# Between out-projection and MLP of a hybrid decoder block: inputs in two sets of tiles, first MLP products among the last transposes, sums by operand, copies in a pool of their own

## The chip, the cores and the metric

The kernel runs on one core of a Trainium2 chip. The metric is the device time of one execution in microseconds. The profile is that of one execution, and its times are counted from the start of the profiled span. PE is TensorE (matmuls, and PEld its weight loads), DVE is VectorE, ACT is ScalarE, POOL is GpSimd, SP is SyncE, which here only issues DMAs.

## The reference

One decoder layer on x of 1024 rows (SEQ) by 1024 channels (D_MODEL), all in float32, with D_FF = 4096:

```python
def reference(x, ...):
    for l in range(DEPTH):            # DEPTH = 1
        h = rms_norm(x, norm_mix[l])
        x = x + hybrid_mixer(h, ...)  # ends with  y @ w_out
        h = rms_norm(x, norm_mlp[l])
        x = x + jnp.square(jax.nn.relu(h @ w_up[l])) @ w_down[l]
    return rms_norm(x, norm_final)
```

The mixer projects h to eight groups, runs two recurrences over the rows (RG-LRU and HGRN2), gates and adds their outputs to y, and multiplies y by w_out. The change concerns what lies between that multiplication and the first product of the MLP.

## The kernel before

**Precision.** A float32 operand is split in two fp32r parts: ACT copies it to the high part "H", DVE subtracts to get the low part "L" (`split`, L86 to L88). A product is three matmuls, H x H, L x H and H x L (`mm3`, L130 to L134).

**Products of the gates and the MLP.** Three stages (gates, MLP up, MLP down) use a recursive scheme with seven products in place of eight. The weights come in quads, 16 for each stage. A quad is loaded as two raw tiles of 512 KB (`load_quad`, L900). `quad_steps` (L905) makes its seven operands: "sums" adds four blocks on DVE into two more raw tiles s; "a" splits block A11 into the pool w1; "b", "c" and "d" split pairs of operands (s1 and s2, s3 and s4, A12 and A22) into tiles "w". There are four raw tiles (pool wp, tag raw) and six tiles w, which out-projection's weights use too. PLAN (L885) names for each step 0 to 6 the PSUM bank (X, Y, Z), the weight operand and the input operand: steps 0, 2, 4 and 6 accumulate in X, 1 and 5 in Y, 3 in Z. A product of one step is 12 matmuls of 128x512. After steps 0, 1 and 2 ACT copies the bank to a tile e; after steps 3, 4 and 5 DVE adds bank and copy into a tile b; after 6 the bank is the result.

**Stages in order.** (1) First norm and the mixer, eight interleaved stages (L873 to L883). (2) The remaining gates, quads 2 to 15 (L1072 to L1121), which read seven input operands: B11, B21 and B22 lie in memory already, t1, n2, T3 and T4 are loaded from DRAM by `load_combo`. `in_turn` chains these loads and the raw loads of the first quads on SP's queue. The gates write y to DRAM (yd). (3) Out-projection of the first 512 rows (`out_proj(0, ...)`, L1129), which reads y tiles loaded by `y_tiles(yp, 0)` and writes x2 to DRAM. (4) Out-projection of the other 512 rows, in two parts of two row tiles each (L1171 to L1193), with the second norm. (5) MLP up (`hidden`, L1215, and `hidden_ops`, L1240), quads 0 to 15. (6) MLP down and the last norm.

**The part around the change.** Row tiles tt = 0 to 3 stand for the rows of both halves: half 0 is row tile tt (loaded from DRAM as x2a), half 1 is row tile 4 + tt (x2s, just made by out-projection). In profile and prediction "tile 2" or "tile 3" is tt. `second_norm(tt, half)` (L1143) scales the row tile (`norm_rows`, L151: ACT squares and sums, DVE adds eps, POOL takes the power, DVE scales into xn), transposes it on PE in two groups of four 128x128 blocks (L1161, PSUM tag hg with two banks), copies the result on ACT to braw (L1162) and splits it into B11 and B21 (half 0) or B22 (half 1). At half 1 it also calls `combos` (L891: four additions on DVE), whose results are split into t1, n2, T3 and T4. Each input operand of the MLP thus has 512 columns, of which each tt makes 128, and a product needs all four. In (4) each part calls `second_norm(tt, 0)` for its two tiles, then two column halves hf of matmuls with eight weight tiles (`next_w`), adds the residual (L1190), stores x2 and calls `second_norm(tt, 1)`. x2a has one buffer. All of y's second half is read from four 1 MB tiles in the pool y1p.

After (4) the pools n2 and y1p close, and w1, ust and up open in their memory. Then quads 0 and 1 are loaded, A11 split, and steps 0 and 3 of both run first (L1256 to L1265); "c" of quad 0 and "sums" of quad 1 come at step 3, "b" and "c" of quad 1 after steps 5 and 6 of quad 0.

**What sets the order.** Each engine executes its instructions in a fixed order. The Tile framework's scheduler sets that order when the kernel is built, by program order as the priority and an estimate of when each instruction can run; `tc.high_priority(n)` moves instructions ahead, and `pin` (L126) keeps PE instructions in program order where `pinned[0]` is set. A tile of a pool that takes the memory of a closed pool waits for the last use of the tiles that lay there (`reuse_waits="tile"`).

Of the kernel before, what the change touches and what calls it, by code (L numbers as in the profile page):

```python
# [10 lines left out]
F32 = mybir.dt.float32  # L11
# [7 lines left out]
P = 128  # L19
# [25 lines left out]
def trunk(ctx: ExitStack, tc: tile.TileContext, x, wts, mlp, pv, gains, mask_f, mask_u, out):  # L45
# [358 lines left out]

    def conv(c, p, xc, xps):
        for s in range(2):
            u = 2 * p + s
            xp = xps[s]
            V.tensor_copy(xp[:, 0:3], xcar[:, u, :])
            for j in range(3):  # L410
                V.scalar_tensor_tensor(  # L411
                    xc[:, s, :],
                    xp[:, j : j + T],
                    pvt[:, PV_CW + 8 * j + u : PV_CW + 8 * j + u + 1],
                    xc[:, s, :],
                    op0=ALU.mult,
                    op1=ALU.add,
                )
            if c + 1 < NC:
# [79 lines left out]
    def hgrn(c, p, got, go):  # L499
# [111 lines left out]
        mul(pairs(kk)[:, :, 0, :], pairs(kc)[:, :, 0, :], t8[:, :, 1:2].to_broadcast([P, 16, 32]))  # L611
        mul(pairs(qf)[:, :, 1, :], q8[:, :, 1, :], t8[:, :, 0:1].to_broadcast([P, 16, 32]))
        level_blocks(0, c0, pt2)
# [145 lines left out]
    def stage(i):  # L759
# [19 lines left out]
        def convolve():  # L779
            got["xc"] = conv(c, p, xc, xps)  # L780

# [123 lines left out]
    def quad_steps(i, pools, raws=raw_tile, minus=False):  # L905
# [22 lines left out]
        def pair(src, names):  # L928
            def go():
                h, lo = (pools[1].tile([P, 1024], F32R, tag="w", name=f"w{names[0]}{i}{q}", bufs=6) for q in "HL")  # L930
# [128 lines left out]
    def ykt(c, ku):  # L1059
        p, s = divmod(ku, 2)  # L1060
        t = yt[c][p]
        s = s if c == 0 else 1 - s
        return t[:, 0, s, :], t[:, 1, s, :]

    def load_combo(o):
        for q in range(2):
            in_turn(gop[o][q].bitcast(F32), cd[o][:, q])
# [4 lines left out]
    for q in own[:2]:  # L1072
        load_quad(GQ + q, dma=in_turn if q == own[0] else load_late)
        gwork[q] = quad_steps(GQ + q, (w1p, wp), minus=True)
        with tc.high_priority(600):
            gwork[q]["a"]()
            if q == own[0]:
                gwork[q]["sums"]()
                gwork[q]["d"]()
    for o in ("t1", "n2"):  # L1080
        load_combo(o)
    in_turn(raw_q[GQ + own[1]][1], mlp[GQ + own[1], 1])
    for o in ("T3", "T4"):
        load_combo(o)
    pinned[0] = True
    for step in (0, 3):
        gate_step(own[0], step)
    pinned[0] = False
    gwork[own[0]]["b"]()
    gwork[own[0]]["c"]()  # L1090
# [3 lines left out]
    for q in own:  # L1094
        n = q + 1
        if n > own[1] and n < QUADS:
            gwork[n] = quad_steps(GQ + n, (w1p, wp), minus=True)
        for step in (1, 2, 4, 5, 6) if q == own[0] else (0, 1, 2, 3, 4, 5, 6):
# [4 lines left out]
            if q == own[0] and step == 2:  # L1103
                gate_step(own[1], 0)
# [13 lines left out]
            for k in {2: ("sums", "a", "b"), 5: ("c",), 6: ("d",)}.get(step, ()):  # L1118
                if q > own[0] or k != "a":
                    gwork[n][k]()  # L1120
        gate_work(q)  # L1121
    close_gp()
    close_tp()
    close_w1()
    close_hB()
    y1p, close_y = opened("y1p")
    y_tiles(y1p, 1)
    xsp, close_xs = opened("xs")
# [5 lines left out]
    HOME = {"T4": 0, "B22": 0, "T3": 0, "B21": 1, "n2": 2, "t1": 2, "B11": 3}  # L1134
    n2p, close_n2 = opened("n2")
    gain1 = gain_tile(1)
# [6 lines left out]
    def second_norm(tt, half):  # L1143
        cut = slice(tt * P, (tt + 1) * P)
        b = braw[tt, half] = n2p.tile([P, 2, T], F32, tag=f"b{half}", name=f"braw{tt}{half}", bufs=2 - half)
        t = tt + 4 * half
        xn = n2p.tile([P, D], F32, tag="xn", name=f"xn_h{t}", bufs=2)
        if half == 0:
            xs = n2p.tile([P, D], F32, tag="x2a", name=f"x2a{t}")
            nc.sync.dma_start(xs, x2d[t])  # L1150
        else:
            xs = x2s[tt]
        norm_rows(xs, xn, gain1, f"h{t}")

        def op_split(src, o):
            split(src.rearrange("p (k t) -> p k t", k=4), hop[o][0][:, :, cut], hop[o][1][:, :, cut])

        for h in range(2):
            pt = bank("hg", f"xT_h{t}_{h}")
            for k in range(4):  # L1160
                PE.transpose(pt[:, k * P : (k + 1) * P], xn[:, (4 * h + k) * P : (4 * h + k + 1) * P], ident)  # L1161
            A.copy(b[:, h, :], pt)  # L1162
            if (half, h) != (1, 0):
                op_split(b[:, h, :], {(0, 0): "B11", (0, 1): "B21", (1, 1): "B22"}[half, h])
        if half == 1:
            b0 = braw[tt, 0]
            combos(b0[:, 0, :], b0[:, 1, :], b[:, 1, :], b[:, 0, :])
            for src, o in ((b0[:, 0, :], "t1"), (b[:, 1, :], "n2"), (b[:, 0, :], "T3"), (b0[:, 1, :], "T4")):
                op_split(src, o)

    for part in range(2):  # L1171
# [5 lines left out]
        for hf in range(2):  # L1177
            pp = {tt: bank("pj", f"po1{hf}{tt}") for tt in tts}
            for j in range(4):
                wh, wl = next_w()  # L1180
                for k in range(2):
                    ku = 2 * j + k
                    yh, yl = ykt(1, ku)
                    cols = slice(k * 512, (k + 1) * 512)
                    for tt in tts:
                        cut = slice(tt * P, (tt + 1) * P)
                        mm3(pp[tt], yh[:, cut], yl[:, cut], wh[:, cols], wl[:, cols], ku == 0, ku == 7)
            for tt in tts:
                cols = slice(hf * 512, (hf + 1) * 512)
                V.tensor_tensor(out=x2s[tt][:, cols], in0=pp[tt], in1=x2s[tt][:, cols], op=ALU.add)  # L1190
        for tt in tts:
            nc.sync.dma_start(x2d[4 + tt], x2s[tt])
            second_norm(tt, 1)  # L1193
    close_n2()
    close_y()


    w1p, close_w1 = opened("w1")
    ust, close_ust = opened("ust")
    up, close_up = opened("up")  # L1200
    U_GROUPS = (("B11", "B21"), ("B22",), ("t1", "T4"), ("n2", "T3"))
    u_d = {
# [4 lines left out]
    u_ops = {}  # L1207
    work, b_of, bank_of, e_of = {}, {}, {}, {}

# [5 lines left out]
    def hidden(q, step):  # L1215
        bk, wo, ho = PLAN[step]
        first = (q, bk) not in bank_of
        if first:
            bank_of[q, bk] = bank(BANK[bk], f"u{bk}{q}")
        if q not in b_of:  # L1220
            b_of[q] = up.tile([P, 4, T], F32, tag="b", name=f"b{q}", bufs=2)
        o, b = bank_of[q, bk], b_of[q]
        wh, wl = ops_w[q][wo]
        hh, hl = hop[ho]
        for k in range(4):
            cols = slice(k * P, (k + 1) * P)
            mm3(o, wh[:, cols], wl[:, cols], hh[:, k, :], hl[:, k, :], first and k == 0, k == 3, not first)
        if step < 3:
            e_of[q, step] = up.tile([P, T], F32, tag="e", name=f"e{step}_{q}", bufs=4)
            A.copy(e_of[q, step], o)  # L1230
# [24 lines left out]

    for q in (0, 1):  # L1256
        load_quad(q)
        work[q] = quad_steps(q, (w1p, wp))
        work[q]["a"]()
        if q == 0:  # L1260
            work[0]["sums"]()
        work[q]["d"]()
        hidden(q, 0)
        hidden(q, 3)
    work[0]["b"]()  # L1265
    for q in range(QUADS):
# [3 lines left out]
        for step in range(7):  # L1270
            if q < 2 and step in (0, 3):
                if q == 0 and step == 3:
                    work[0]["c"]()
                    work[1]["sums"]()
                continue
            hidden(q, step)
            if q == 0:
                if step > 4:
                    work[1]["b" if step == 5 else "c"]()
                continue  # L1280
            if step == 1:
# [9 lines left out]
    late_u, close_late_u = opened("late_u", side="right")  # L1291
    hidden_ops(QUADS - 1, late_u, (2, 5), True)
    close_up()
    acc0, close_acc0 = opened("acc0", side="right")
# [170 lines left out]
```

## Time and profile before

| | |
|---|---|
| three runs of the kernel before | 1588.41 us median (1586.48 to 1588.73) |
| the profiled execution, its own time | 1585.07 us |
| its span | 1583.3 us |
| granted TensorE clock, mean | 0.992 |
| PE, DVE, ACT, POOL busy | 97%, 76%, 52%, 10% |
| DMA | 280.07 MB, mean 177 GB/s |

By stage PE's row of the 40 slices looks like this (a digit is the busy share of a slice of 39.6 us in tenths):

```profile
PE   7989999999999999999999978999999999999998
DVE  5797586696876938686856488988778888888877
```

The mixer takes the first 580 us, the gates 580 to 846, the out-projection of the first half 846 to about 893, the out-projection of the second half with the second norm up to 942, the MLP the rest. A row of the timeline reads: start, duration, engine, line, operation, output <- inputs, sizes, count, and in brackets how long the engine stood idle before it and what ended the wait. A row of the busy time by stage reads: stage, its length, busy time (instructions) of PE, PEld, DVE, ACT and POOL, granted TensorE clock, DMA share, GB/s. Matmul durations overlap, since matmuls are pipelined.

### The profile page before, as it was taken

What the parts mean: (1) busy time and instruction counts of PE and PEld (TensorE: products, weight loads), DVE (VectorE), ACT (ScalarE), POOL (GpSimd) and SP (SyncE); (2) the same over time, 40 slices, a digit from 0 to 9 for tenths busy, and PEclk for the clock granted to TensorE, in tenths of its full rate; (3) what the DMA queues carried; (4) which work ended last, traced back from release to release, by engine and by line L of the source; (5) the groups of instructions that cost most, each with busy time, mean ns of one, the idle gap of its engine ahead of it and who ended that gap; (6) DMA issues with size and microseconds to landing.
All of it is one profiled execution on the core that took longest, in us unless ns stands there. A gap on an engine that the chain in (4) does not pass through costs nothing.

```text
span 1583.3 us, 23131 instructions
## 1 busy us (share of the span) xinstructions
PE 1531.4 (97%) x9072; PEld 1278.8 (81%) x9072; DVE 1209.5 (76%) x1706; ACT 820.8 (52%) x1341; POOL 162.6 (10%) x187
## 2 busy tenths in 40 slices
PE   7989999999999999999999978999999999999998
PEld 6878888888788888888888767888888878888886
DVE  5797586696876938686856488988778888888877
ACT  5656756557475534454533376777677632211113
POOL 1021110234436600000000000000000000000000
PEclk9999999999999999999999999999999999999999
DMA  6223122232343375332328762766666675666652
GB/s 241 96 94 107 67 103 85 94 121 94 134 137 118 106 269 199 130 117 96 134 95 310 260 212 80 279 253 252 253 249 248 226 273 226 246 255 254 254 199 107
DMA packets 72205, 280.07 MB, mean 177 GB/s; under 512 B 7712, under 2 KB 16032, under 8 KB 59168
## 3 DMA queue, kind: packets, MB, share of 16 engines
q1 hardware_dynamic: 69072, 267.58, 45.3%
q10 hardware_dynamic: 3024, 11.01, 1.9%
q8 instruction: 71, 1.16, 0.3%
q14 instruction: 38, 0.31, 0.1%
HBM read 193.63 MB, written 84.93 MB: 176 GB/s over the span
## 4 chain that ended last, share of the span: by engine, by line
PE 76%; DVE 13%; ACT 6%; issue 2%; DMA 2%; POOL 1%; DVEq 0%; SPq 0%; POOLq 0%; ACTq 0%
PE dX L132 3%; PE dX L133 3%; PE uX L132 3%; PE dX L134 3%; PE uX L134 3%; PE gX L134 3%; PE gX L133 3%; PE uX L133 3%; PE gX L132 3%; PE uY L134 2%; PE gY L134 2%; PE gY L133 2%; PE uY L132 2%; PE uY L133 2%; PE gY L132 2%
## 5 line engine op out<-in xcount | busy, mean ns | idle before, releaser
L88 DVE TENSOR_TENSOR wL<-raw,wH 128x1024 fp32r<-128x1024 f32 x100 | 124.3, 1245 | 91.4 <-ACT wH L87 89.9
L87 ACT CAST wH<-raw 128x1024 fp32r<-128x1024 f32 x100 | 105.0, 1050 | 71.2 <-PE po L133 36.6
L1374 DVE TENSOR_TENSOR acc<-acc,dX 128x512 f32<-128x512 f32 x128 | 85.1, 685 | 29.3 <-PE dX L134 28.7
L87 ACT CAST wA<-q 128x512 fp32r<-128x512 f32 x46 | 28.4, 621 | 132.6 <-PE dX L134 101.4
L1374 DVE TENSOR_TENSOR acc<-acc,dY 128x512 f32<-128x512 f32 x64 | 43.5, 686 | 15.7 <-PE dY L134 14.5
L133 PE MATMUL po<-wL,y 128*128 128x512 f32 x128 | 50.0, 391 | 0.0
L134 PE MATMUL po<-wH,y 128*128 128x512 f32 x128 | 50.0, 391 | 0.0
L132 PE MATMUL po<-wH,y 128*128 128x512 f32 x128 | 49.8, 389 | 0.0
L1234 ACT ACTIVATE b<-b 128x512 f32<-128x512 f32 x48 | 30.2, 632 | 35.7 <-DVE b L1233 35.7
L155 POOL TENSOR_TENSOR rstd_h<-rstd_h,mhalf 128x1 f32<-128x1 f32 x8 | 5.5, 687 | 385.1 <-DVE rstd_h L154 385.1
L411 DVE SCALAR_TENSOR_TENSOR xc<-xp,pvt,xc 128x512 f32<-128x512 f32 x48 | 40.4, 864 | 0.0
L710 ACT ACTIVATE on<-po 128x128 f32<-128x128 f32 x64 | 16.9, 278 | 44.9 <-PE po L706 44.9
L88 DVE TENSOR_TENSOR wA<-q,wA 128x512 fp32r<-128x512 f32 x46 | 31.5, 686 | 10.3 <-ACT wA L87 10.3
L324 POOL TENSOR_TENSOR stt<-r,stt 128x256 fp32r<-128x256 f32 x16 | 23.2, 1467 | 93.1 <-ACT stt L323 93.1
L915 DVE TENSOR_TENSOR s<-q,q 128x512 f32<-128x512 f32 x46 | 31.6, 688 | 1.2 <-DMA q<-mlp_in 0.7
L920 DVE TENSOR_TENSOR s<-q 128x512 f32<-128x512 f32 x46 | 31.6, 687 | 0.4
L1235 ACT ACTIVATE b<-b 128x512 f32<-128x512 f32 x48 | 30.1, 631 | 1.1
L132 PEld LDWEIGHTS po<-wH,y 128*128 128x128 f32 x128 | 24.0, 188 | 5.0
L134 PEld LDWEIGHTS po<-wH,y 128*128 128x128 f32 x128 | 24.0, 188 | 4.9
L133 PEld LDWEIGHTS po<-wL,y 128*128 128x128 f32 x128 | 24.0, 188 | 4.9
L703 PE MATMUL po<-v,scT 128*128 128x128 f32 x128 | 24.7, 286 | 2.8 <-DVE sn L689 2.8
L616 POOL TENSOR_SCALAR scT<-dd 32x256 f32<-32x256 f32 x32 | 22.0, 687 | 50.4 <-DVE dd L532 48.9
(2528 smaller groups left out, 5422.6 us busy)
## 6 DMA issues: line engine op xcount, KB each, us to landing
raw<-wts_in SPq DMA_DIRECT2D x96, 512.0 KB, 3.4
q<-mlp_in SPq DMA_DIRECT2D x92, 512.0 KB, 3.5
y<-yd SPq DMA_DIRECT2D x7, 1024.0 KB, 8.7
x<-x_in SPq DMA_DIRECT2D x8, 512.0 KB, 6.0
hd<-ri SPq DMA_DIRECT2D x16, 256.0 KB, 2.7
od<-onT ACTq DMA_DIRECT2D x8, 512.0 KB, 4.4
cdT<-stT SPq DMA_DIRECT2D x16, 256.0 KB, 3.3
o<-od SPq DMA_DIRECT2D x4, 1024.0 KB, 7.3
```

Of the source, the lines that this page charges most:

```text
L87: keep(A.copy(h, src))
L88: keep(V.tensor_tensor(out=lo, in0=src, in1=h.bitcast(F32), op=ALU.subtract))
L132: pin(PE.matmul(o, ah, bh, start=first, stop=False, **how))
L133: pin(PE.matmul(o, ah, bl, start=False, stop=False, **how))
L134: pin(PE.matmul(o, al, bh, start=False, stop=last, **how))
L411: V.scalar_tensor_tensor(xc[:, s, :], xp[:, j : j + T], pvt[:, PV_CW + 8 * j + u : PV_CW + 8 * j + u + 1], xc[:, s, :], op0=ALU.mult, op1= ...
L703: pin(PE.matmul(on_ps, scT[:, 4 * s + n, :], vn(s, n), start=True, stop=only))
L915: V.tensor_tensor(out=sa[:, 0, :], in0=a21, in1=a22, op=ALU.add)
L920: V.tensor_tensor(out=sb[:, 0, :], in0=a21, in1=a11, op=ALU.add)
L1234: A.activation(b[:, at, :], b[:, at, :], AF.Relu, scale=-1.0 if at == 2 else 1.0)
L1235: A.activation(b[:, at, :], b[:, at, :], AF.Square)
L1374: V.tensor_tensor(out=dst, in0=dst, in1=banks[bk, pr], op=op)
```

## The change

- **Gates, first quads:** for quad 2 (the first) "b" is made ahead of "d" and under the same high priority, and the loads of t1, n2 and T3 stand ahead of the raw loads of quad 3. Quad 2's steps run in the order 1, 2, 5, 4, 6, and quad 3's first product follows step 4. The work on quad 3's operands gets a high priority.
- **Pools:** w1 and n2 open ahead of y1p and ahead of the out-projection.
- **Inputs in two sets:** y of the second half is loaded in eight tiles of 256 rows, four for part 0 (in n2) and four for part 1 (in y1p), instead of four tiles of 512 rows. Tiles that part 0 has read serve tt = 2 and 3 as x2a and as xn.
- **Norms:** the transposed rows are copied back into xn, braw has no tiles of its own; transposes are pinned where `pinned[0]` is set.
- **Sums by operand:** the four additions and the splits of t1, n2, T3 and T4 move from `second_norm` to a generator; they run after all four tiles' norms, t1 of every tile first, then n2, T3, T4.
- **Last part:** at part 1, hf 1, PE runs weights 0 and 1 for both tiles, then 2 and 3 for tile 2, then 2 and 3 for tile 3, pinned. Ahead of the last tile's matmuls `first_weights` loads quads 0 and 1 and makes "a" of both and "sums" and "b" of quad 0. After the matmuls PE runs product (quad 0, step 0), tile 2's transposes, product (quad 1, step 0), tile 3's transposes.
- **MLP start:** then "d" and "c" of quad 0 at high priority, and the steps of quad 0 in the order 3, 1, 2, 5, 4, 6, pinned, without those of quad 1, whose operands follow. The copies e get a pool `ep` of their own.
- `conv` gets a parameter that is None wherever it is called, and `got["wide"]` is stored and not read.

```diff
@@ second_norm
-        b = braw[tt, half] = n2p.tile([P, 2, T], F32, tag=f"b{half}", ...)
+        late = half == 0 and tt > 1
-        xn = n2p.tile([P, D], F32, tag="xn", name=f"xn_h{t}", bufs=2)
...
-            xs = n2p.tile([P, D], F32, tag="x2a", name=f"x2a{t}")
+            xs = n2p.tile([P, D], F32, tag=f"y0{2 * tt - 4}" if late else "x2a", name=f"x2a{t}")
...
+        home = {2: "y01", 3: "y03", 5: "x2a", 6: "y00", 7: "y02"}.get(t, "xn")
+        xn = n2p.tile([P, D], F32, tag=home, name=f"xn_h{t}", bufs=3 if home == "xn" else 1)
         norm_rows(xs, xn, gain1, f"h{t}")
+        b = braw[tt, half] = xn.rearrange("p (h t) -> p h t", h=2)
...
+        def operands():
+            b0 = braw[tt, 0]
+            b11, b21, b22, b12 = b0[:, 0, :], b0[:, 1, :], b[:, 1, :], b[:, 0, :]
+            V.tensor_tensor(out=b11, in0=b11, in1=b12, op=ALU.subtract)
+            op_split(b11, "t1")
+            yield
+            V.tensor_tensor(out=b12, in0=b22, in1=b12, op=ALU.subtract)
+            V.scalar_tensor_tensor(b22, b11, -1.0, b22, op0=ALU.mult, op1=ALU.subtract)
+            op_split(b22, "n2")
+            yield
+            op_split(b12, "T3")
+            yield
+            V.scalar_tensor_tensor(b21, b22, -1.0, b21, op0=ALU.mult, op1=ALU.subtract)
+            op_split(b21, "T4")
+            yield
...
+    def first_weights():
+        for q in (0, 1):
+            load_quad(q)
+            work[q] = quad_steps(q, (w1p, wp))
+            work[q]["a"]()
+            if q == 0:
+                work[0]["sums"]()
+                work[0]["b"]()
...
+            turn = [(j, tts) for j in range(4)]
+            if (part, hf) == (1, 1):
+                turn = turn[:2] + [(j, tts[i : i + 1]) for i in range(2) for j in (2, 3)]
+                pinned[0] = True
+            w = {}
+            for n, (j, those) in enumerate(turn):
+                if j not in w:
+                    w[j] = next_w()
+                if n == 4:
+                    first_weights()
...
-        for tt in tts:
+        for i, tt in enumerate(tts):
+            if part:
+                product(i, 0)
             nc.sync.dma_start(x2d[4 + tt], x2s[tt])
-            second_norm(tt, 1)
+            rest.append(second_norm(tt, 1))
+    rest_of_it()
...
+    with tc.high_priority(400):
+        work[0]["d"]()
+        work[0]["c"]()
+    for q, step in ((0, 0), (1, 0), (0, 3), (0, 1), (0, 2), (0, 5), (0, 4), (0, 6)):
+        with tc.high_priority(300):
+            hidden(q, step)
+        if (q, step) == (0, 2):
+            work[1]["sums"]()
+    pinned[0] = False
+    work[1]["b"]()
+    work[1]["c"]()
+    work[1]["d"]()
+    hidden_ops(0, ust, (1, 3), False)
```

`product(q, step)` is the matmul part of `hidden`; for steps (0, 0) and (1, 0) `hidden` then only copies the bank.

More of the change, by code (lines that the diff above doesn't have):

```diff
@@ L403, in conv_in, with conv @@
         return xc, xps
-    def conv(c, p, xc, xps):
+    def conv(c, p, xc, xps, behind=None):
         for s in range(2):
@@ L1102, in trunk @@
             gate_step(q, step)
-            if q == own[0] and step == 2:
+            if q == own[0] and step == 4:
                 gate_step(own[1], 0)
@@ L1125, in trunk @@
     close_hB()
+    w1p, close_w1 = opened("w1")
+    n2p, close_n2 = opened("n2")
     y1p, close_y = opened("y1p")
-    y_tiles(y1p, 1)
+    for part, pool in enumerate((n2p, y1p)):
+        yt[1, part] = [pool.tile([P, 2, 2, 2 * P], F32R, tag=f"y{part}{p}", name=f"y1{part}{p}") for p in range(NPAIR)]
+    for part in range(2):
+        for p in range(NPAIR):
+            rows = slice(2 * part * P, 2 * (part + 1) * P)
+            nc.sync.dma_start(yt[1, part][p].bitcast(F32), yd[p][:, :, 2:4, rows])
     xsp, close_xs = opened("xs")
@@ L1164, in second_norm, with rest_of_it, product @@
                 op_split(b[:, h, :], {(0, 0): "B11", (0, 1): "B21", (1, 1): "B22"}[half, h])
[L1165 removed]
+        def operands():
             b0 = braw[tt, 0]
[L1167 to L1169 removed]
+            b11, b21, b22, b12 = b0[:, 0, :], b0[:, 1, :], b[:, 1, :], b[:, 0, :]
[11 more added lines that the diff above has]
+            yield
+        return operands()
+    rest = []
+    def rest_of_it():
+        for _ in range(4):
+            for one in rest:
+                next(one)
+    work, b_of, bank_of, e_of = {}, {}, {}, {}
+    def product(q, step):
+        bk, wo, ho = PLAN[step]
+        first = (q, bk) not in bank_of
+        if first:
+            bank_of[q, bk] = bank(BANK[bk], f"u{bk}{q}")
+        o = bank_of[q, bk]
+        wh, wl = ops_w[q][wo]
+        hh, hl = hop[ho]
+        for k in range(4):
+            cols = slice(k * P, (k + 1) * P)
+            mm3(o, wh[:, cols], wl[:, cols], hh[:, k, :], hl[:, k, :], first and k == 0, k == 3, not first)
+        return o
+    def first_weights():
[6 more added lines that the diff above has]
+                work[0]["b"]()
     for part in range(2):
@@ L1215, in hidden @@
     def hidden(q, step):
[L1216 to L1219, printed above, removed]
+        o = bank_of[q, "X"] if q < 2 and step == 0 else product(q, step)
         if q not in b_of:
             b_of[q] = up.tile([P, 4, T], F32, tag="b", name=f"b{q}", bufs=2)
[L1222 to L1227, printed above, removed]
+        b = b_of[q]
         if step < 3:
-            e_of[q, step] = up.tile([P, T], F32, tag="e", name=f"e{step}_{q}", bufs=4)
+            e_of[q, step] = ep.tile([P, T], F32, tag="e", name=f"e{step}_{q}", bufs=4)
             A.copy(e_of[q, step], o)
@@ L1269, in trunk @@
             work[n] = quad_steps(n, (w1p, wp))
[L1270 to L1275, printed above, removed]
+        for step in range(q == 1, 7):
             hidden(q, step)
[L1277 to L1280, printed above, removed]
             if step == 1:
```

69 lines of the change are left out of this document (34 added, 35 removed).

## The prediction

> **What bounds the kernel now.** I read the busy shares first, then busy time by stage, then the waits of PE and the timelines of the stages that are not full.
>
> ```profile
> PE 1531.4 (97%) x9072; PEld 1278.8 (81%) x9072; DVE 1209.5 (76%) x1706; ACT 820.8 (52%) x1341; POOL 162.6 (10%) x187
> 560.00:600.00 40.00, 40.00 (x191) 33.48 (x190) 11.83 (x15) 15.01 (x40) 1.65 (x1) 1.00 0.84 316
> 904.00:985.40 81.40, 66.79 (x306) 53.00 (x305) 68.11 (x98) 54.85 (x90) 5.49 (x8) 0.94 0.46 161
> 1400.00:1500.00 100.00, 100.00 (x443) 82.84 (x442) 79.47 (x112) 22.72 (x24) 0.00 (x0) 1.00 0.58 227
> ```
>
> A stage row gives length, then PE, PEld, DVE, ACT and POOL busy with counts, then granted clock, DMA share, GB/s. PE bounds the kernel, so an edit can win only where PE stands still or slow. Where it is full, 443 matmuls take 100 us, 0.226 each. The gates' start (560 to 600) has no gap. Between out-projection and MLP, 904 to 985.4 (the end of quad 0's last product), 306 PE instructions run: 64 transposes and 242 matmuls. Eight transposes delay the next matmul by 0.82 us (921.84 and 922.66 below), (eight sets), so the work is 242 x 0.226 + 8 x 0.82 = 61.3 us, and **20.1 us are lost** in 81.4. That is the purse.
>
> ```profile
> 921.84 1.06 PE L1161 MATMUL xT_h<-ident,xn_h 128*128 128x128 f32 x8 [0.34 <-ACT h2B21H L87]
> 922.66 0.49 PE L134 MATMUL po<-wH,y 128*128 128x512 f32 x1
> 942.07 0.39 PE L134 MATMUL po<-wH,y 128*128 128x512 f32 x1
> 942.88 1.06 PE L1161 MATMUL xT_h<-ident,xn_h 128*128 128x128 f32 x8 [0.42 <-DVE xn_h L156]
> 950.19 1.94 PE L1161 MATMUL xT_h<-ident,xn_h 128*128 128x128 f32 x8 [6.25 <-DVE rstd_h L154]
> 956.17 0.40 PE L133 MATMUL uX<-h2B11L,wA 128*128 128x512 f32 x1
> 959.90 0.50 PE L134 MATMUL uX<-h2B11H,wA 128*128 128x512 f32 x1 [0.40 <-DVE wA L88]
> 963.59 0.50 PE L132 MATMUL uZ<-h2B21H,wA120H 128*128 128x512 f32 x1 [1.08 <-ACT braw L1162]
> 976.73 0.50 PE L132 MATMUL uX<-h2T3H,ws30H 128*128 128x512 f32 x1 [1.97 <-ACT ws30H L87]
> 942.50:950.10 7.60, 1.06 (x8) 0.86 (x8) 7.13 (x14) 4.30 (x8) 0.86 (x1) 0.72 0.53 207
> 950.10:954.10 4.00, 3.47 (x16) 3.13 (x17) 3.57 (x6) 2.75 (x6) 0.85 (x1) 0.50 0.36 131
> 954.10:956.20 2.10, 2.10 (x7) 1.48 (x7) 1.38 (x4) 2.10 (x5) 0.54 (x1) 0.54 0.46 137
> 974.70:976.70 2.00, 0.07 (x1) 0.00 (x0) 0.00 (x0) 1.98 (x4) 0.00 (x0) 1.00 0.00 0
> ```
>
> I split it at these rows. **The hole:** out-projection ends at 942.30; at 956.17 the clock is full again. In those 13.87 us lie three sets of transposes and four matmuls, 3.4 us of work: 10.5 lost, 2.9 of them because the clock stands at half after the 6.25 us gap (950.1 to 956.2 is 6.1 us, and holds 3.2 us of work). **956.17 to 963.59:** 20 matmuls and eight transposes, 5.3 of 7.4: 2.1 lost (A11 of quad 1; a PSUM bank of the transposes). **963.59 to 985.4:** seven products of 12 matmuls, 19.0 of 21.8: 2.8 lost, for "c" of quad 0. The remaining **4.8** lie before 942.30, at four sets of transposes, 1.2 each.
>
> ```profile
> 941.45 1.28 DVE L156 SCALAR_TENSOR_TENSOR xn_h<-x2a,rstd_h,gain 128x1024 f32<-128x1024 f32 x1
> 942.76 0.33 SPq L1150 DMA_DIRECT2D x2a<-x  x1
> ```
>
> Why the hole: tile 2's scaling waits in DVE's queue until 941.45, behind the sums of tiles 0 and 1; tile 3's load is issued only after it (one buffer), and its transposes are those of 950.19.
>
> **Part by part, inputs and norms.** Computing instructions are neither added nor removed, except that L1190, the splits and the norms change places; `conv` gets None and `wide` is read nowhere: nothing. The four 1 MB loads of y become eight of half that, 4 more issues on SP at 0.33 to 0.5 us each, while out-projection's first half keeps PE busy. Out-projection's part 1 reads its own tiles, so part 0's fall free during its second half, and tiles 2 and 3 load into them without waiting for each other; their norms stand ahead of all sums. On SP these two loads then stand ahead of the loads of the MLP's weights, and wait for PE's last read of a y tile instead of DVE's scaling. So their transposes move among the out-projection matmuls. The hole closes: **-10.5**. Each of the two moved sets costs a wait there as its four neighbours did: **+2.4** (bounds 0, and 2 x 2.0 by the worst row, 1.77 idle and restart).
>
> ```profile
> 918.11 1.06 PE L1161 MATMUL xT_h<-ident,xn_h 128*128 128x128 f32 x8 [1.77 <-DVE xn_h L156]
> 934.88 0.68 DVE L1190 TENSOR_TENSOR x2s<-po,x2s 128x512 f32<-128x512 f32 x1
> 914.67 1.06 ACT L153 ACTIVATE xn_h<-x2a 128x1024 f32<-128x1024 f32 x1 [1.60 <-DMA x2a<-x]
> 916.09 0.56 POOL L155 TENSOR_TENSOR rstd_h<-rstd_h,mhalf 128x1 f32<-128x1 f32 x1 [8.14 <-DVE rstd_h L154]
> ```
>
> **First products among the last transposes.** From the end of tile 2's matmuls its chain is the add 0.68, square 1.06, POOL 0.56, scaling 1.28, and some 0.65 for the read-out, the small DVE step and the signals: 4.2 us. PE has tile 3's last 12 matmuls (2.7) and product(0) (2.7) to do: 5.4, covered. Tile 3's chain starts 2.7 later, with product(0), transposes and product(1), 6.2, as cover. If a product is late, its cover is gone and the chain shows.
>
> The new wait is **product(1), pinned in PE's order**: behind it stand tile 3's transposes and everything of the MLP. It needs A11 of quad 1, whose raw tile is loaded when quad 0's sums free a buffer:
>
> ```profile
> SPq L903 <- DVE s L919: 5.2, 1, 5.2
> 955.45 0.64 ACT L87 CAST wA<-q 128x512 fp32r<-128x512 f32 x1
> 959.16 0.68 DVE L88 TENSOR_TENSOR wA<-q,wA 128x512 fp32r<-128x512 f32 x1
> 950.03 0.68 DVE L919 TENSOR_TENSOR s<-s,q 128x512 f32<-128x512 f32 x1
> 950.78 28.89 SPq L903 DMA_DIRECT2D q<-mlp_in  x4
> q<-mlp_in SPq DMA_DIRECT2D x92, 512.0 KB, 3.5
> ```
>
> Behind that waiting load on SP stand the stores of x2, which nobody needs before the MLP's end. Now the sums come before the last adds and norms, so I take A11 as in time, and its old 0.6 (0.40 and restart) as won: **-0.6**. The bank wait behind tile 3's transposes stays (1.08 and restart).
>
> **Sums by operand, copies in their own pool.** "b" and "c" of quad 0 come early: **-2.8**. The copies of X no longer wait for the norms' memory; if they did, they would now be late, since PE comes to the second product on X sooner. But (0,4) and (0,6) both write X, and now follow each other: PE must wait for the DVE add that reads X. One add 0.68, the matmul's tail 0.16 (0.39 less 0.226), signals and restart some 0.35: **+1.2** (bounds 0, if a product of quad 1 slips between, and 2.4, if the add queues behind a 1.2 us split like ws334L below).
>
> PE alone: -10.5 + 2.4 - 0.6 - 2.8 + 1.2 = **-10.3**; PE would be done with T4's product at 972.4, before Z of quad 1 (2.7).
>
> **DVE decides the rest.**
>
> ```profile
> 905.40:945.00 39.60, 34.12 (x167) 27.20 (x165) 34.79 (x49) 28.24 (x45) 3.24 (x5) 1.00 0.64 223
> 945.00:972.30 27.30, 20.19 (x86) 16.14 (x87) 25.67 (x41) 17.57 (x32) 2.25 (x3) 0.81 0.27 99
> 985.40:1004.00 18.60, 18.60 (x83) 15.24 (x82) 18.07 (x24) 14.84 (x22) 0.00 (x0) 1.00 0.64 254
> 971.07 0.69 DVE L88 TENSOR_TENSOR h2T4L<-braw,h2T4H 128x512 fp32r<-128x512 f32 x1
> ```
>
> From 905.4 to the last T4 it works 60.5 us; without 2.3 of quad 1 and with "c" (1.2) 59.4. Keeping the 4.8 us of gaps before 945, T4 is ready at 969.6, which is when PE wants it (972.4 less 2.7). So no wait yet, but quad 1's four sums (2.8) and "b" (1.2) come behind it, and after 985.4 DVE is 97% busy already. It removes gaps only: 13 us of them stand in 905.4 to 1004 (4.8, 1.6, 6.1 and 0.5), of which the first two I expect to stay: 6.6 of gain if PE waited for every DVE result, 10.3 if for none. I take the middle, **+1.8**.
>
> **Gates.** Quad 3's raw halves now load behind T3, ahead of T4:
>
> ```profile
> 586.66 0.50 SPq L962 DMA_DIRECT2D gT4L<-cdT  x1
> gT4L<-cdT SPq DMA_DIRECT2D x1, 1024.0 KB, 9.7
> 580.48 1.23 DVE L88 TENSOR_TENSOR ws334L<-s,ws334H 128x1024 fp32r<-128x1024 f32 x1 [3.09 <-ACT ws334H L87]
> 596.55 0.39 PE L132 MATMUL gY<-hT11H,ws334H 128*128 128x512 f32 x1
> 599.27 0.39 PE L132 MATMUL gX<-gT4H,wA1234H 128*128 128x512 f32 x1
> ```
>
> T4 landed at 596.4 and is used at 599.27. One MB more at 316 GB/s is 3.3 us: 599.7 at worst. The swapped steps 4 and 5, with quad 3's first product behind them, ask for "c" (ws3) two products ahead of 596.55 instead of one, at 591.1, and it has been split since 581.7; quad 3's A11 is asked for later than now. I take 0 (bounds 0 and 0.8; nothing to win, PE is full there).
>
> Sum: -10.3 + 1.8 = **-8.5 us**. The profiled execution is 1585.07 us (span 1583.3), so 1576.6; the runs' median is 1588.41 (1586.48 to 1588.73), 3.3 above it, so I forecast **1580.0** on that footing, 0.60, with its own range 1576 to 1584.
>
> **Rivals.**
>
> ```profile
> 904.76 0.69 DVE L1190 TENSOR_TENSOR x2s<-po,x2s 128x512 f32<-128x512 f32 x1 [1.29 <-DMA x2s<-x_in]
> 955.55 1.28 DVE L156 SCALAR_TENSOR_TENSOR xn_h<-x2s,rstd_h,gain 128x1024 f32<-128x1024 f32 x1 [0.72 <-POOL rstd_h L155]
> ```
>
> *More goes:* the loads into memory that is free earlier also spare the 4.8 and the 2.4 of waits in the out-projection; DVE's 13 us of gaps are the ceiling. -8.5 - 4.8 - 2.4 would be -15.7, so taken as -13: 1575.4. For: L1190 waited for x2s once, 1.29. Against: the order that makes the waits is static. 0.10.
> *DVE becomes the bound:* as it fills, the splits of quad 1 arrive late and new gaps open behind PE. Half of the 8.5 stays: 1584.2. For: 97% after 985.4. 0.08.
> *It doesn't do what it says:* tile 3's norm stays behind other DVE work, so the hole stays; only -2.8 + 1.2 remain: 1586.8. Against: the sums that blocked it now come last. 0.08.
> *Slower:* product(1) waits for A11. By my sum PE reaches it at 942.3 + 1.6 + 2.4 + 2.7 + 0.8 = 949.8 (the two moved sets, their waits, product(0), tile 2's transposes). Ready is the third of quad 0's sums plus 5.1 (load 3.5, cast 0.64, split 0.68, signals). A wait over 6 us also halves the clock, 2.9 as in the hole. The gain is gone when it is ready at 957.2, that is, when that sum ends at 952.1 (before: 950.7), and 0.2% are lost from 955.3 on. If the sums queue behind tile 3's scaling (before: to 956.8, the last row above), the third ends at 958.6, A11 is ready at 963.7, and the time is 1588.4 + 13.9 + 2.9 - 10.3 = **1594.9** (DVE catches up meanwhile, so 10.3 counts and not 8.5). Against: the sums stand earlier now. 0.14.
> [...]
>
> **Chances and range.** 0.2% (3.2 us) is about what a measurement of this kernel can tell from no change. Faster: 0.60 + 0.10 + 0.08 = 0.78; same 0.08; slower 0.14. The range 1573 to 1589 takes in the DVE bounds and all but the slower case and the tail below.
>
> **What would show it.** Right: no PE gap over 2 us from 904 on, clock 1.00 throughout, tile 2's and 3's transposes between out-projection matmuls, DVE above 95% there. Wrong: PE waiting for A11 of quad 1 or ahead of (0,6) for more than 2.4 us; a DVE wait of quad 1's products; PE gaps at 599.

## The result and the profile after

The changed kernel takes **1581.78 us** (median of six runs, 1579.99 to 1582.82), the kernel before 1587.16 in the runs beside it: a ratio of 0.9965, 95% interval 0.9954 to 0.9976. The profiled execution is 1579.99 us, 5.1 less than the one of before. Three rows of PE's timeline cut each execution in the same way: the first product of the gates, their last one, the first product of MLP down. They are from before, then from after:

```profile
580.13 0.48 PE L132 MATMUL gX<-hT00H,wA 128*128 128x512 f32 x1
846.56 0.39 PE L134 MATMUL gX<-gT4H,wA1247L 128*128 128x512 f32 x1
1264.62 0.39 PE L132 MATMUL dX<-wA,u14B 128*128 128x512 f32 x1
```
```profile
579.24 0.48 PE L132 MATMUL gX<-hT00H,wA 128*128 128x512 f32 x1
850.83 0.39 PE L134 MATMUL gX<-gT4H,wA1247L 128*128 128x512 f32 x1
1259.79 0.39 PE L132 MATMUL dX<-wA,u14B 128*128 128x512 f32 x1
```

The gates take 266.4 us before and 271.6 after: **5.2 lost**. From there to MLP down, which holds all that lies between out-projection and MLP, it is 418.1 and 409.0: **9.1 won**. What lies ahead and behind differs by 0.9 and 0.3. These two lengths are the measure for every run below, since the start of the gates moves by up to 7 us from one profile to the next and the gates' length, where nothing in them is changed, by 0.02.

**Where the 9.1 came from.** Busy time by stage after, in the columns of the prediction; 947.70 is just ahead of the first product of the MLP (947.73):

```profile
904.00:985.40 81.40, 73.44 (x346) 58.37 (x345) 73.62 (x103) 58.08 (x94) 5.21 (x8) 1.00 0.49 171
904.00:947.70 43.70, 40.41 (x200) 32.76 (x199) 38.27 (x50) 30.71 (x48) 3.50 (x6) 1.00 0.67 228
```

By the prediction's own count the 346 instructions are 64 transposes and 282 matmuls, 282 x 0.226 + 8 x 0.82 = 70.3 us of work: 11.1 of the 81.4 us are lost now, 20.1 before. Up to 947.70 it is 152 matmuls and six sets, 39.3 of 43.7, so 4.4 are lost there and 6.7 behind it. The clock is at 1.00 throughout, and the hole is gone. Transposes, the first products and what PE waits for in the timeline of after:

```profile
929.73 1.06 PE L1182 MATMUL xT_h<-ident,xn_h 128*128 128x128 f32 x8
...
933.85 1.06 PE L1182 MATMUL xT_h<-ident,xn_h 128*128 128x128 f32 x8 [1.43 <-ACT h2B21H L87]
...
952.99 1.06 PE L1182 MATMUL xT_h<-ident,xn_h 128*128 128x128 f32 x8 [2.38 <-DVE rstd_h L154]
953.81 0.49 PE L132 MATMUL uX<-h2B11H,wA 128*128 128x512 f32 x1
...
956.68 1.03 PE L1182 MATMUL xT_h<-ident,xn_h 128*128 128x128 f32 x8
...
965.57 0.50 PE L132 MATMUL uX<-h2n2H,ws10H 128*128 128x512 f32 x1 [0.27 <-ACT h2n2H L87]
```

Tile 2's and 3's first transposes (929.73, 933.85) stand among the out-projection's matmuls. At the end tile 2's set waits 2.38 us, product(1) at 953.81 and tile 3's set at 956.68 for nothing.

**Where the 5.2 went.** Loads on SP, then DVE, then PE, then busy time by stage in the gates of after:

```profile
584.20 1.73 SPq L969 DMA_DIRECT2D q<-mlp_in  x2
...
598.42 3.30 SPq L969 DMA_DIRECT2D q<-mlp_in  x2
```
```profile
593.21 0.69 DVE L1000 TENSOR_TENSOR gb<-gY,ge 128x512 f32<-128x512 f32 x1 [6.86 <-PE gY L134]
...
595.86 0.69 DVE L1000 TENSOR_TENSOR gb<-gX,ge 128x512 f32<-128x512 f32 x1 [1.36 <-PE gX L134]
596.46 0.68 DVE L918 TENSOR_TENSOR s<-q,q 128x512 f32<-128x512 f32 x1
...
605.39 0.69 DVE L918 TENSOR_TENSOR s<-q,q 128x512 f32<-128x512 f32 x1 [2.26 <-DMA q<-mlp_in]
...
618.49 0.68 DVE L1000 TENSOR_TENSOR gb<-gX,ge 128x512 f32<-128x512 f32 x1
```
```profile
619.22 0.50 PE L132 MATMUL gX<-gT4H,wA1235H 128*128 128x512 f32 x1 [2.74 <-DVE gb L1000]
```
```profile
617.00:619.20 2.20, 0.00 (x0) 0.00 (x0) 2.20 (x4) 0.59 (x1) 0.00 (x0) 1.00 0.90 331
619.20:620.20 1.00, 0.98 (x4) 0.84 (x5) 1.00 (x2) 1.00 (x3) 0.00 (x0) 0.98 0.80 221
620.20:623.40 3.20, 3.20 (x9) 2.43 (x9) 2.90 (x2) 0.23 (x1) 0.00 (x0) 0.50 0.22 87
```

The same rows of before:

```profile
555.75 0.34 SPq L962 DMA_DIRECT2D q<-mlp_in  x1
...
576.21 0.33 SPq L962 DMA_DIRECT2D q<-mlp_in  x1
...
588.91 5.54 SPq L962 DMA_DIRECT2D q<-mlp_in  x2
```
```profile
586.97 0.68 DVE L915 TENSOR_TENSOR s<-q,q 128x512 f32<-128x512 f32 x1
...
615.64 0.68 DVE L993 TENSOR_TENSOR gb<-gX,ge 128x512 f32<-128x512 f32 x1
```

Read it backwards. PE's last product of quad 3 writes X again, and must wait for the DVE addition that reads X. That addition starts 2.85 us later than before (618.49 against 615.64), because in DVE's order it stands, with no gap between, behind an operation that had waited 2.26 us, until 605.39, for a raw tile of quad 4. Quad 4's two tiles were asked for from 598.42 on instead of from 588.91, because they need buffers that quad 3's sums free (SP stands 10.5 us ahead of them, until the sum of L920), and these sums began at 596.46 instead of 586.97. Two things made the sums late. Quad 3's own raw tiles were asked for from 584.20 on, behind T3, instead of at 555.75 and 576.21. And the sums now stand in DVE's order behind the additions at 593.21 and 595.86, for which DVE waited 6.86 and 1.36 us on PE, although the tiles had landed by 590.6 at the latest (the second was issued by 585.6, and the slowest of these loads took 5.0 us). PE's 2.74 us and 1.6 of the 3.2 us at clock 0.50 are 4.3 of the 5.2; the rest was not traced.

### The profile page after: what moved, and what is told of

Its sections match the earlier page's. It is cut to its first block, busy times and chain, and to the rows that moved or that the text cites. A ratio compares the mean times of both kernels' runs of the same rounds, so it can differ in the third digit from the quotient of the medians.

```text
span 1578.2 us, 23146 instructions
## 1 busy us (share of the span) xinstructions
PE 1528.8 (97%) x9072; PEld 1275.6 (81%) x9072; DVE 1208.0 (77%) x1706; ACT 819.6 (52%) x1341; POOL 162.0 (10%) x187
## 4 chain that ended last, share of the span: by engine, by line
PE 75%; DVE 14%; ACT 7%; issue 2%; DMA 1%; POOL 0%; DVEq 0%; POOLq 0%; SPq 0%; ACTq 0%
PE dX L132 3%; PE dX L133 3%; PE dX L134 3%; PE uX L132 3%; PE uX L133 3%; PE uX L134 3%; PE gX L132 3%; PE gX L134 3%; PE gX L133 3%; PE dY L132 2%; PE dY L133 2%; PE dY L134 2%; PE uY L132 2%; PE uY L134 2%; PE uY L133 2%
## 5 line engine op out<-in xcount | busy, mean ns | idle before, releaser
L1000 DVE TENSOR_TENSOR gb<-gY,ge 128x512 f32<-128x512 f32 x14 | 9.7, 690 | 26.0 <-PE gY L134 25.4
```

## The experiments

Theory: the part between out-projection and MLP gives its 9 us by itself; the gates lose 5 by the order of loads. Rivals: the gates' loss goes with the new norm order, or comes from the swapped steps. The kernel before ran beside each group again (medians 1587.5 to 1587.9), and the ratios are to those runs. The last two columns are the lengths defined above, from one profile each; "half" marks the profiles in which the clock fell to half behind the 2.4 us wait of tile 2's last transposes, which costs 1.6 us (last section).

| run | us, median | ratio to before, 95% interval | gates | to MLP down |
|---|---|---|---|---|
| before | 1587.16 | | 266.4 | 418.1 |
| after | 1581.78 | 0.9965 [0.9954, 0.9976] | 271.6 | 409.0 |
| gates_undone | 1577.55 | 0.9937 [0.9920, 0.9953] | 266.4 | 409.1 half |
| gates_alone | 1591.30 | 1.0022 [1.0010, 1.0034] | 271.1 | 418.8 |
| loads_back | 1577.59 | 0.9938 [0.9915, 0.9961] | 266.4 | 408.2 |
| steps_back | 1578.66 | 0.9944 [0.9922, 0.9965] | 268.7 | 409.7 half |
| splits_behind | 1579.14 | 0.9943 [0.9927, 0.9959] | 266.4 | 410.7 |
| one_buffer | 1577.76 | 0.9940 [0.9925, 0.9955] | 266.4 | 408.4 |
| sums_early | 1583.22 | 0.9978 [0.9968, 0.9987] | 266.4 | 413.5 |
| products_behind | 1581.48 | 0.9964 [0.9951, 0.9977] | 266.4 | 411.4 |
| shared_pool | 1585.52 | 0.9990 [0.9979, 1.0002] | 266.4 | 413.5 |
| sums_early_one_buffer | 1585.99 | 0.9998 [0.9987, 1.0008] | 266.4 | 413.9 |
| sums_on_gpsimd | 1580.57 | 0.9956 [0.9943, 0.9970] | 266.4 | 413.7 half |
| sums_left_out | 1577.13 | 0.9940 [0.9917, 0.9963] | 266.4 | 408.6 half |

**The gates.** gates_undone takes all four edits in the gates back (loads, "b", steps, priority); gates_alone puts these four, and nothing else, into the kernel before. loads_back and steps_back are the changed kernel with one of them undone:

```diff
@@ loads_back
-                for o in ("t1", "n2", "T3"):
-                    load_combo(o)
+    for o in ("t1", "n2"):
+        load_combo(o)
     in_turn(raw_q[GQ + own[1]][1], mlp[GQ + own[1], 1])
-    load_combo("T4")
+    for o in ("T3", "T4"):
+        load_combo(o)
@@ steps_back
-        for step in (1, 2, 5, 4, 6) if q == own[0] else (0, 1, 2, 3, 4, 5, 6):
+        for step in (1, 2, 4, 5, 6) if q == own[0] else (0, 1, 2, 3, 4, 5, 6):
...
-            if q == own[0] and step == 4:
+            if q == own[0] and step == 2:
```

> The changed kernel with all four edits of the gates taken back (loads, b ahead of d, step order, priorities). Load theory and step theory alike: the 2.74 us wait of PE in the gates and the half clock after it go, the gates take 5 us less, the span is near 1573 us and the time 0.993 to 0.994 of the kernel before. Rival, the loss in the gates is chance or comes from elsewhere (memory, code): the wait stays, 0.9965 of before.

> The kernel before with the four edits of the gates and nothing else. Load and step theory: a PE wait of 2.5 to 3 us near 619 us with half clock after it, some 4 to 5 us slower than before (1.003). Rival (not the gates' edits): no wait, 1.000.

> The changed kernel with only the order of the loads as before (quad 3's second raw half ahead of T3, first half ahead of t1); step order, b ahead of d and priorities stay. Load theory (quad 3's raw halves wait behind T3, so quad 4's load is late, DVE stands 2.3 us waiting for it, and the add that reads bank X comes late): no wait of PE in the gates, span near 1573. Step theory: the wait stays, span near 1578.

> The changed kernel with only the order of the steps as before (1, 2, 4, 5, 6 and quad 3's first product behind step 2); the loads stay as changed. Load theory: the wait of PE in the gates stays, 2 to 4 us, or moves earlier, since A11 of quad 3 is now asked for 5 us sooner; span 1578 or more. Step theory: it goes, span near 1573.

The two parts add up: the gates take 271.1 us with the four edits alone and 266.4 without them, whatever the norms do, and the rest is 418.8 and 409.1. By the medians gates_alone loses 3.5 us and gates_undone gains 10.3. With only the loads put back the gates are at 266.4 as well, so steps, priority and the early "b" cost nothing once the loads are in time. With only the steps put back 2.3 are lost, in other places:

```profile
PE gX L132 <- ACT wA L87: 1.2, 1, 1.2
PE gX L132 <- DVE gb L1000: 0.3, 1, 0.3
```

These are PE's waits in the gates of steps_back: quad 3's A11 is late for its first product, which the old order of steps wants sooner. There quad 4's tiles are asked for 4.5 us sooner than in after, and DVE doesn't wait for them:

```profile
593.94 2.63 SPq L969 DMA_DIRECT2D q<-mlp_in  x2
```

So the moved loads are the cause, since nothing is lost without them; but with them the new steps lose 2.9 us more than the old ones (5.2 against 2.3). The early "b" and the priority were not tried alone. gates_undone and loads_back beat both kernels; the gain of the part between out-projection and MLP is all of theirs.

**What made the hole.** one_buffer loads all four tiles of half 0 into one x2a again; sums_early puts each tile's sums back behind its norms; the third run does both. All stand on gates_undone.

```diff
@@ one_buffer
-            xs = n2p.tile([P, D], F32, tag=f"y0{2 * tt - 4}" if late else "x2a", name=f"x2a{t}")
+            xs = n2p.tile([P, D], F32, tag="x2a", name=f"x2a{t}")
@@ sums_early
-            rest.append(second_norm(tt, 1))
-    rest_of_it()
+            for _ in second_norm(tt, 1):
+                pass
```

> The gates as before the change, and all four tiles of the first half's norms load into one buffer again (sums still last). Theory: the hole had two causes, and the buffer is one: tile 3's load must wait for tile 2's scaling, its transposes move towards the end of the out-projection, and PE loses 3 to 8 us. Rival: what made the hole was only the sums in DVE's queue ahead of the scaling; then tile 3's load still goes early enough and the time stays within 1 us of gates_undone's 1577.55.

> The gates as before the change, and each tile's sums right behind its norms again (own buffers kept). Theory that the order of the sums made the hole: tiles 2 and 3's norms queue behind the sums of tiles 0 and 1 on DVE, PE waits again over 3 us for a set of transposes and the time is 3 to 8 us over gates_undone's 1577.55. Rival, that the buffer alone made it: the loads go early, the norms come in time, and the time stays within 1 us.

> The gates as before the change, each tile's sums right behind its norms, and one buffer for the loads of the first half's norms. Theory: the sums' place is the cause, and the buffer prolongs the wait when the sums stand ahead: from the last gate product to the first down product it takes 416 to 420 us (sums_early 413.5, before 418.1), with a PE wait of over 5 us ahead of a set of transposes. Rival: the buffer never matters here, and it takes within 0.7 us of sums_early's 413.5.

With the sums last, one buffer costs nothing (408.4; the medians are 1577.76 and 1577.55). The place of the sums is worth 4.4 to 6.0: 413.5 less 409.1, or less 407.5, which is an estimate of gates_undone without its half clock. By the medians it is 5.7. In the profile of sums_early the clock fell to half twice, behind waits of 2.46 and 2.88 us.

Whether the buffer costs something when the sums are early stays open. The two profiles say 413.9 against 413.5, as the rival had it; the medians say 1585.99 against 1583.22, with intervals that only touch. A wait of over 5 us came with both put back, as the theory had it, at half clock (the set behind it takes 1.94 us instead of 1.06), but ahead of tile 3's last transposes and not of its first ones as before (PE's timeline of sums_early_one_buffer):

```profile
963.98 1.94 PE L1180 MATMUL xT_h<-ident,xn_h 128*128 128x128 f32 x8 [6.00 <-DVE xn_h L156]
```

**The cover and the pool.** products_behind runs both first products behind the last transposes; shared_pool takes the copies e from the pool of b, in the norms' memory.

```diff
@@ products_behind
-            if part:
-                product(i, 0)
...
+        if part:
+            product(0, 0)
+            product(1, 0)
@@ shared_pool
-            e_of[q, step] = ep.tile([P, T], F32, tag="e", name=f"e{step}_{q}", bufs=4)
+            e_of[q, step] = up.tile([P, T], F32, tag="e", name=f"e{step}_{q}", bufs=4)
```

> The gates as before the change, and the first product of quads 0 and 1 behind both last tiles' transposes, not among them. Theory that they cover the norms' chain: PE's wait ahead of tile 2's transposes grows from 2.4 by the 2.7 us of a product to about 5, the clock falls to half behind it (some 2.9 us), and the time is 5 to 8 us over gates_undone's 1577.55. Rival: DVE, which is nearly full there, sets the end of T4's split anyway, the products fill later gaps, and the time is under 2 us longer.

> The gates as before the change, and the copies "e" back in the pool of "b", whose memory is the norms'. My step in the prediction: the copies of X would then wait for the norms' memory and be late, so PE waits ahead of its second product on X; from the last gate product to the first down product it takes 3 to 7 us more than the 409.1 of gates_undone. Rival: the scheduler puts other products in between, or DVE sets the pace there anyway, and it takes under 1 us more.

Both cost. PE's rows of products_behind, then of shared_pool:

```profile
954.71 1.94 PE L1180 MATMUL xT_h<-ident,xn_h 128*128 128x128 f32 x8 [5.10 <-DVE rstd_h L154]
957.09 2.02 PE L1180 MATMUL xT_h<-ident,xn_h 128*128 128x128 f32 x8 [0.45 <-DVE xn_h L156]
```
```profile
967.99 0.80 PE L132 MATMUL uX<-h2n2H,ws10H 128*128 128x512 f32 x1 [7.98 <-ACT e L1294]
```

The wait and the half clock came as expected (5.10, sets of 1.94 and 2.02), but only 2.3 to 3.9 us are lost (3.9 by the medians), under the 5 to 8 and over the rival's 2. Part was made up later: PE's waits behind the transposes, 1.3 us in gates_undone, are gone from this trace. Without a pool of its own the copy of X goes into the norms' memory, and comes only at 967.36, right behind the last of T4's casts (966.83) on ACT; PE stands 7.98 us ahead of the second product on X. Of it 4.4 to 6.0 us remain in this profile, which is the second fastest of its ten runs, and 8.0 by the medians.

**Is DVE what PE waits for?** splits_behind orders DVE's splits of quad 0's "d" and "c" behind tile 2's scaling. sums_on_gpsimd moves the subtractions that make T3 to GpSimd; sums_left_out leaves them out.

```diff
@@ splits_behind
+        if after_it[0] is not None:
+            how = mybir.DependencyInfo(mybir.DependencyClass.NoSync, mybir.DependencyReason.DATA)
+            tc.add_manual_dep(ins.ins, after_it[0].ins.name, how, reason="after_it")
@@ sums_on_gpsimd
-            V.tensor_tensor(out=b12, in0=b22, in1=b12, op=ALU.subtract)
+            G.tensor_tensor(out=b12, in0=b22, in1=b12, op=ALU.subtract)
```

> The gates as before the change, and the splits of quad 0's "d" and "c" ordered on DVE behind tile 2's last scaling. Theory: PE's 2.38 us wait for tile 2's transposes is long because two splits of 1.2 us stand ahead of the chain's own DVE instructions; with them behind it the wait falls to about 0.6 us and the time by about 1.8 us under gates_undone's 1577.55. Rival: the splits come due right behind, so PE then waits for quad 0's ws operands at Z or Y instead, and the time stays within 0.5 us of gates_undone.

> The gates as before the change, and the four subtractions that make T3 (0.69 us each on DVE) on GpSimd, which is almost idle there. Theory: after product(0) DVE sets the pace (one gap of 0.44 us from 941 to 972 in gates_undone), so taking 2.8 us from it gives 1.5 to 2.8 us between the last gate product and the first down product (409.1 in gates_undone). Rival: PE's own waits have other causes (signals and chains), or GpSimd's slower subtraction makes T3 late: within 0.5 us, or longer.

> The gates as before the change, and the four subtractions that make T3 left out altogether: T3 is then made from the plain quarter, so the output's values are others, while 2.8 us of DVE work go and no other engine takes them. Theory that DVE sets the pace in this stretch: 1.5 to 2.8 us less between the last gate product and the first down product than gates_undone's 409.1. Rival: what PE still waits for there are chains through several engines, and DVE is full beside them without being waited for: 1.0 us less at most.

In splits_behind the wait of 2.38 did fall, to 0.71, but ahead of the second product on X the gain is given back:

```profile
949.10 1.06 PE L1187 MATMUL xT_h<-ident,xn_h 128*128 128x128 f32 x8 [0.71 <-DVE xn_h L162]
...
963.34 0.50 PE L138 MATMUL uX<-h2n2H,ws10H 128*128 128x512 f32 x1 [1.48 <-ACT h2n2H L89]
```

That product starts 17.8 us behind the first one (945.51), exactly as in after (947.73 to 965.57). So the wait moved, as the rival said, though to the cast of n2 and not to quad 0's weights; the median is 1.6 us over gates_undone's, where the rival allowed 0.5, but their intervals overlap. sums_left_out, set against gates_undone (both "half"), gives 0.56 us for 2.8 us of DVE work: in after DVE is busy 94% of the time behind 947.70 (35.35 of 37.70 us), yet PE waits for little of these four subtractions. sums_on_gpsimd made the stretch 4.6 longer in its profile, which is the longest of its five runs, and by the medians some 3 longer than gates_undone. The cause is in GpSimd's and DVE's rows:

```profile
928.48 1.29 POOL L1191 TENSOR_TENSOR xn_h<-xn_h 128x512 f32<-128x512 f32 x1
...
965.43 3.43 POOL L1191 TENSOR_TENSOR xn_h<-xn_h 128x512 f32<-128x512 f32 x1 [4.30 <-ACT h2B22H L87]
```
```profile
925.03 1.29 DVE L156 SCALAR_TENSOR_TENSOR xn_h<-x2s,rstd_h,gain 128x1024 f32<-128x1024 f32 x1 [0.66 <-POOL rstd_h L155]
...
928.55 2.31 DVE L156 SCALAR_TENSOR_TENSOR xn_h<-x2a,rstd_h,gain 128x1024 f32<-128x1024 f32 x1 [0.43 <-POOL rstd_h L155]
```

The scaling that runs beside a GpSimd subtraction takes 2.31 us instead of 1.29 (begun 0.07 us behind the subtraction, it ends 1.09 us after it), and it was tile 2's first one (PE's next set waits 0.93 and the one behind it 2.44, against 0 and 1.43 in gates_undone, and the clock fell to half behind the 2.44); the subtraction of 965.43, beside DVE's work until 967.70, takes 3.43 instead of 1.29. What prolongs them side by side no row shows.

## Why the prediction was right and where it failed

The sign and the size between out-projection and MLP were right (8.5 forecast, 9.1 measured), but the size in part by luck: the two moved sets cost 2.8 us less than forecast, and tile 2's chain, forecast as covered, made a wait of 2.38. The step that failed is **"Gates … I take 0 (bounds 0 and 0.8; nothing to win, PE is full there)"**: it measured 5.2, and loads_back shows the load order as its cause. The prediction priced the moved loads by T4's landing alone, and T4 was in time. What it left out was the load that the others were moved past: quad 3's raw tiles, 8 to 28 us later on SP, the sums that need them, the buffers that these sums free, quad 4's tiles behind those, and the DVE queue in which an instruction waiting for quad 4 stands ahead of the addition that frees X. It took the swapped steps as harmless by asking when "c" and A11 are wanted; steps_back shows that, beside the late loads, they cost 2.9 of the 5.2. "Quad 3's A11 is asked for later than now" was true and looked at one consumer of quad 3's tiles; the sums are the other. The prediction named PE gaps at 599 as the sign of being wrong here; the gap came at 616 to 619.

The other steps:

- **The hole, -10.5.** Closed: no wait over 2.38 from 904 on, clock 1.00. Of its two reasons the sums' place is shown; the single buffer costs nothing once the sums are last, and beside early sums its part is open.
- **Two moved sets, +2.4.** Up to the first product 4.4 us are lost where 4.8 + 2.4 = 7.2 were expected. Tile 2's set at 929.73 waits for nothing and tile 3's 1.43; the other four sets wait 1.9 in all, where they waited 4.0 before.
- **Tile 2's chain, covered.** It was not: 2.38 and a restart. Add, square and scaling took what was said, and the power 0.85 instead of 0.56; but the chain took 7.8 us, from the end of tile 2's matmuls (945.17) to its transposes (952.99), instead of 4.2 (in which the 0.65 for read-out, small DVE step and signals was the author's estimate; read-out and step take 0.19 and 0.14 here). The rest is DVE's queue. The add waits for the split of quad 0's "b" ahead of it, and between add and scaling stand two more splits of quad 0, one of quad 1, another tile's add and another tile's subtraction; program order puts that subtraction behind all norms, but the scheduler set it here. DVE of after:

```profile
945.49 1.23 DVE L88 TENSOR_TENSOR ws10L<-s,ws10H 128x1024 fp32r<-128x1024 f32 x1
946.63 0.68 DVE L1264 TENSOR_TENSOR x2s<-po,x2s 128x512 f32<-128x512 f32 x1
947.43 1.22 DVE L88 TENSOR_TENSOR wA120L<-q,wA120H 128x1024 fp32r<-128x1024 f32 x1
948.57 0.68 DVE L1264 TENSOR_TENSOR x2s<-po,x2s 128x512 f32<-128x512 f32 x1
949.17 0.14 DVE L154 TENSOR_SCALAR rstd_h<-rstd_h 128x1 f32<-128x1 f32 x1
949.23 0.68 DVE L1193 TENSOR_TENSOR xn_h<-xn_h 128x512 f32<-128x512 f32 x1
949.83 1.22 DVE L88 TENSOR_TENSOR ws30L<-s,ws30H 128x1024 fp32r<-128x1024 f32 x1
950.97 0.68 DVE L88 TENSOR_TENSOR wA<-q,wA 128x512 fp32r<-128x512 f32 x1
951.57 1.27 DVE L156 SCALAR_TENSOR_TENSOR xn_h<-x2s,rstd_h,gain 128x1024 f32<-128x1024 f32 x1
```

  The scaling could have begun at about 950.3, when the power was there. A chain is not the sum of its links where other work stands between them on the same engine. splits_behind, which moves the two splits of 947.43 and 949.83 away, brings the wait to 0.71. That the cover itself matters products_behind shows.
- **A11 of quad 1, -0.6, and "b" and "c" early, -2.8.** PE's waits for both are gone from the trace; no run tried them alone.
- **Two products on X in a row, +1.2.** Only a short stop (0.49 us instead of 0.23 from the matmul at 974.54 to the next): four matmuls of quad 1 slip between, as the lower bound said. The 0.35 for signals and restart was the author's estimate, without a row; in the gates of after PE starts 0.05 us behind the end of the addition it waited for (618.49 + 0.68, 619.22), and its first two matmuls start 0.34 apart instead of 0.23.
- **The copies' own pool.** The prediction said they would be late in the norms' memory: so it was in shared_pool, 7.98 us of wait.
- **DVE, +1.8.** PE's waits for t1 and n2 in after (in all, times, longest):

```profile
PE uY L133 <- DVE h2t1L L88: 0.8, 1, 0.8
PE uX L133 <- DVE h2n2L L88: 0.7, 1, 0.7
```

  The size is about right (these two and two waits of 0.2 and 0.3 beside them); of DVE's fullness, the four subtractions of sums_left_out cost about 0.6.
- **The slower rival.** product(1) did not wait for A11.

The forecast of 1580.0 lies only 1.8 under the median, and that is luck too: the change in the profile was 3.4 less than forecast (5.1 against 8.5), and the footing of 3.3 above the profiled execution was itself more than these runs show (1.8). By the medians the gain is 5.4 where 8.4 were forecast.

## What to carry to other kernels

When loads are reordered on a queue, price the load that the others were moved past, not only those that moved: follow its buffers to the next load and to the instruction that waits for it, and look at what stands behind that instruction on its engine. A change in PE's order of steps also changes the order on the engines that serve PE: ask what now stands behind an instruction that waits for PE. Where an engine is full and PE has a wait for it, moving its work about may only move the wait, as in splits_behind; count what is still late next. A change of two independent parts is best measured in two lengths of one timeline: here they gave -9.1 and +5.2 where the total said -5. Each length is one execution's, so set it beside the medians.

## What the runs showed of the hardware

**Behind the same wait of 2.4 us the clock is halved in some profiles and not in others.** Eight profiles, each of another of these kernels, have the 2.38 or 2.39 us wait ahead of tile 2's last transposes, with the same matmuls around it. In after, one_buffer and shared_pool the clock stays at 1.00 and the next set comes 3.66 to 3.69 us later, as it does in loads_back (3.66); in gates_undone, sums_on_gpsimd and sums_left_out it falls to 0.50 and the next set comes 5.24 to 5.28 us later, as in steps_back (5.28, the set itself 1.94 instead of 1.06). Busy time by stage of one_buffer, then of gates_undone, 1 to 3 us behind the wait:

```profile
952.09:953.09 1.00, 1.00 (x6) 0.82 (x5) 1.00 (x1) 1.00 (x3) 0.00 (x0) 1.00 0.00 0
953.09:954.09 1.00, 1.00 (x6) 0.80 (x6) 1.00 (x3) 0.90 (x3) 0.00 (x0) 1.00 0.00 0
```
```profile
950.59:951.59 1.00, 1.00 (x4) 0.81 (x3) 1.00 (x1) 1.00 (x3) 0.00 (x0) 0.50 0.00 0
951.59:952.59 1.00, 1.00 (x4) 0.71 (x4) 1.00 (x3) 0.90 (x3) 0.00 (x0) 0.50 0.00 0
```

The prediction reckoned with a halved clock only behind a wait of over 6 us. In these runs it fell behind 2.38 us as well, and behind 2.74 in the gates (0.50 from 620.20 to 623.40), and the same 2.38 also left it at 1.00. What decides in a given execution no run here shows.
